# A two-layer encoder step on one core: down products added into DRAM by accumulating transfers, and stage ends by quarters of the tokens

## The chip, the cores and the metric

One core of a Trainium2 chip runs the whole program. The metric is the device time of one execution in microseconds, the median of several runs. TensorE (PE in the profile) multiplies, VectorE (DVE) and ScalarE (ACT) work elementwise and read the results from PSUM banks, GpSimd (POOL) does elementwise work and issues transfers, and SyncE (SP) issues transfers. Each engine executes its own instructions in order and waits on semaphores for the others.

## The reference

All data are fp32. There are 1024 new tokens of one stream and 32 of another, 1056 together, with a width of 1024.

```python
# layer 0
x = x + mixer(rmsnorm(x, a_norm))        # (gb * dwconv3(gc * u)) @ w_out
x = x + conv_ffn(rmsnorm(x, ffn_norm0))
# layer 1
k, v, logf = rmsnorm(x, kv_norm) @ w_kv   # shared keys, values, forget logits
x = x + fox_attention(rmsnorm(x, b_norm) @ w_q, k, v, logf) @ w_o
x = x + conv_ffn(rmsnorm(x, ffn_norm1))
y = rmsnorm(x, final_norm)

def conv_ffn(h):                          # d_ff = 2816
    g, v = split(dwconv3(h @ w_up), 2)    # causal depthwise convolution, width 3
    return (silu(g) * v) @ w_down
```

## The kernel before, in words

**Data.** The residual x is kept transposed, as eight tiles x[0..7] of 128 channels × 1056 tokens (`NK` = 8, `TT` = 1056). Tokens are cut in three ways: `CH`, three chunks of 352; `HALVES`, two of 528; `ENDS`, four quarters of 264. Each fp32 factor is split in a high part, rounded by ScalarE to the type that TensorE multiplies fast, and a low part, the difference, by VectorE. A product is three matmuls, high·high, high·low and low·high; `chain` (L167, matmuls L173 to L175) does them for a list of inner tiles. `bank` names PSUM: in the feed-forward stages two banks `d` of 512 and three banks `p` of 1024 columns. `keep`, `slot` and the pool for weights hand out SBUF; a tile is handed out again when its readers are done.

**Stages.** Mixer (`mixer`), feed-forward 0 (`ffn(0)`), attention (`attention`), feed-forward 1 (`ffn(1)`) run one behind the other. Norms are computed by `rstd` (L227): the sums of squares over channels by six small matmuls with a vector of ones (L238), a few operations on 88 × 3 numbers (L240 to L245), a diagonal `dg` (L247), a matmul that broadcasts it (L250) and a copy to `rstd` (L251). In the mixer and in attention the last down products call `summed`: for each tile of x and chunk the VectorE add (L321), the square (L224, ScalarE), its sum (L225, GpSimd, or VectorE for the last tile), and the spill of x to DRAM. The norm starts when the last tile is done.

**Feed-forward.** `begin` (L359) applies norm and gain to x by halves (L384), splits it (L374, L375), runs the first two tiles of the up product (L395), and forms the sums f1 to f4 of the quarters of x (L408 to L411) and their splits. From then on `pair` (L501) makes one gate tile and one value tile by seven products instead of eight (`product`, L498, 24 matmuls of 264 columns each, 168 in all); its operands are weights or sums of weights made by GpSimd (L523, L524, L532, L545) and split by `operand` (L487, L488). `act` turns a pair into an activation tile: halo copies by GpSimd (L287), a first convolution product by ScalarE (L296), two more by VectorE (L297, L298), silu (L567), product (L569) and split (L573, L574). There are 22 such tiles (`NF`).

**Down products.** x does not fit in SBUF during a feed-forward stage; it lies in DRAM as `xd`. After every two acts `stream` (L598) takes 24 steps, 8 tiles of x by 3 chunks. Each one loads a chunk of x (L607, on SP), does 6 matmuls, adds the result on VectorE (L610) and stores the chunk (L611, on SP). There are 5 slots `xs`. The steps of one group are set between the seven products of the next two `pair` calls, by a count of matmuls (L587); the last group is half left over when the last pair ends. Then x is loaded, and the last two acts are added by `down` (feed-forward 0) or `finish` (L257), which goes by quarters and writes the normed output. All transfers of weights, x and outputs stand in SP's one queue, in program order.

**Attention.** `weave` sets filler steps between the softmax work of each head; for the last head the fillers are 48 steps of the output product (`down_steps`) for the first six of eight head pairs, and the last two pairs follow.

## Time and profile before

| | us |
|---|---|
| median of 3 runs (lowest, highest) | 2775.31 (2773.56, 2778.65) |
| the profiled execution | 2773.91 |
| its span, first to last instruction | 2772.1 |
| TensorE busy | 2550.4 |
| VectorE busy | 1823.5 |
| ScalarE busy | 1057.2 |
| GpSimd busy | 473.7 |

The span is one execution as the profiler recorded it. "Busy" is the time in which an engine executed something; transfers that it issues and waits are not counted. PEclk is the clock that TensorE was granted, as a share of full speed. The page cuts the span in 40 equal slices and prints the busy share of each in tenths. A wait is named by the engine and line that waited, and by what released it.

### The profile page before, as it was taken

What the parts mean: (1) busy time and instruction counts of PE and PEld (TensorE: products, weight loads), DVE (VectorE), ACT (ScalarE), POOL (GpSimd) and SP (SyncE); (2) the same over time, 40 slices, a digit from 0 to 9 for tenths busy, and PEclk for the clock granted to TensorE, in tenths of its full rate; (3) what the DMA queues carried; (4) which work ended last, traced back from release to release, by engine and by line L of the source; (5) the groups of instructions that cost most, each with busy time, mean ns of one, the idle gap of its engine ahead of it and who ended that gap; (6) DMA issues with size and microseconds to landing.
All of it is one profiled execution on the core that took longest, in us unless ns stands there. A gap on an engine that the chain in (4) does not pass through costs nothing. (4 is left out here: it accounts for less than half of the span.)

```text
span 2772.1 us, 45529 instructions
## 1 busy us (share of the span) xinstructions
PE 2550.4 (92%) x17332; PEld 2471.8 (89%) x17332; DVE 1823.5 (66%) x3266; ACT 1057.2 (38%) x1850; POOL 473.7 (17%) x467
## 2 busy tenths in 40 slices
...
PEclk9999998999999999989999999999899999999997
...
GB/s 109 41 46 46 50 138 24 136 165 172 178 180 180 170 174 178 191 124 47 56 58 50 51 58 58 87 196 128 23 120 168 172 176 175 179 183 176 176 170 121
DMA packets 239786, 341.73 MB, mean 123 GB/s; under 512 B 31952, under 2 KB 195280, under 8 KB 239568
## 3 DMA queue, kind: packets, MB, share of 16 engines
...
## 5 line engine op out<-in xcount | busy, mean ns | idle before, releaser
L498 PE MATMUL pb_p<-b,wb 128*128 128x264 f32 x7056 | 951.1, 287 | 27.4 <-ACT u L530 14.8
L498 PEld LDWEIGHTS pb_p<-b,wb 128*128 128x128 f32 x7056 | 918.9, 190 | 31.8 <-ACT u L530 15.3
L610 DVE TENSOR_TENSOR xs<-xs,pb_d 128x352 f32<-128x352 f32 x480 | 246.9, 519 | 374.5 <-DMA xs<-xd 219.8
L173 PE MATMUL pb_d<-acth,wb 128*128 128x352 f32 (+1 forms) x992 | 331.6, 338 | 52.7 <-DVE xs L610 52.3
L175 PE MATMUL pb_d<-acth,wb 128*128 128x352 f32 (+1 forms) x992 | 326.3, 329 | 4.5 <-DVE wb L488 4.5
L174 PE MATMUL pb_d<-actl,wb 128*128 128x352 f32 (+1 forms) x992 | 324.9, 328 | 0.0
L173 PE MATMUL pb_d<-xh,wh 128*128 128x384 f32 (+2 forms) x864 | 287.4, 336 | 14.0 <-ACT xh L162 7.4
L174 PE MATMUL pb_d<-xl,wh 128*128 128x384 f32 (+2 forms) x864 | 285.6, 331 | 5.8 <-DVE xl L163 5.7
L175 PE MATMUL pb_d<-xh,wl 128*128 128x384 f32 (+2 forms) x864 | 284.8, 330 | 1.0 <-DVE wl L151 0.8
L487 ACT ACTIVATE wb<-wr 128x512 fp32r<-128x512 f32 x210 | 131.9, 628 | 359.5 <-PE pb_p L498 277.1
L173 PEld LDWEIGHTS pb_d<-acth,wb 128*128 128x128 f32 x992 | 190.4, 193 | 70.0 <-DVE xs L610 63.8
L487 ACT ACTIVATE wb<-ws 128x512 fp32r<-128x512 f32 x168 | 105.2, 627 | 295.4 <-PE pb_p L498 157.5
L523 POOL TENSOR_TENSOR ws<-wr 128x512 f32<-128x512 f32 x42 | 56.5, 1346 | 884.9 <-DMA wr<-in_w_up 438.0
L175 PEld LDWEIGHTS pb_d<-acth,wb 128*128 128x128 f32 x992 | 191.9, 193 | 6.2 <-DVE wb L488 6.2
L174 PEld LDWEIGHTS pb_d<-actl,wb 128*128 128x128 f32 x992 | 192.3, 194 | 0.2
L173 PEld LDWEIGHTS pb_d<-xh,wh 128*128 128x128 f32 x864 | 166.1, 193 | 20.0 <-ACT xh L162 7.9
L150 ACT ACTIVATE wh<-wraw 128x1024 fp32r<-128x1024 f32 (+1 forms) x71 | 74.3, 1046 | 275.8 <-PE pb_o L174 138.6
L174 PEld LDWEIGHTS pb_d<-xl,wh 128*128 128x128 f32 x864 | 166.7, 193 | 8.1 <-DVE xl L163 7.7
L175 PEld LDWEIGHTS pb_d<-xh,wl 128*128 128x128 f32 x864 | 166.3, 193 | 2.7 <-DVE wl L151 2.5
L488 DVE TENSOR_TENSOR wb<-wr,wb 128x512 fp32r<-128x512 f32 x210 | 161.8, 770 | 4.0 <-ACT wb L487 3.5
L296 ACT ACTIVATE y<-u,cv 128x1058 f32<-128x1058 f32 x96 | 108.5, 1175 | 80.8 <-POOL u L287 80.7
L859 DVE TENSOR_TENSOR pt<-pb_d,pt 128x512 fp32r<-128x512 f32 (+1 forms) x160 | 99.0, 632 | 60.4 <-ACT pt L858 59.3
(289 smaller groups left out, 4628.0 us busy)
## 6 DMA issues: line engine op xcount, KB each, us to landing
xs<-xd SPq DMA_DIRECT2D x480, 176.0 KB
xd<-xs SPq DMA_DIRECT2D x480, 176.0 KB
wr<-in_w_up SPq DMA_DIRECT2D x168, 256.0 KB
wr<-in_w_down SPq DMA_DIRECT2D x84, 256.0 KB
...
```

The lines of the kernel that those rows point to most:

```text
L150: nc.scalar.activation(h[:, i:j], raw[:, i:j], AF.Copy)
L173: nc.tensor.matmul(ps, wh, xh[:, c[0]:c[1]], start=(i == 0), stop=False)
L174: nc.tensor.matmul(ps, wh, xl[:, c[0]:c[1]], start=False, stop=False)
L175: nc.tensor.matmul(ps, wl, xh[:, c[0]:c[1]], start=False, stop=(i == n - 1))
L296: nc.scalar.activation(y, u[:, 0:TC], AF.Copy, scale=w[:, 0:1])
L487: nc.scalar.activation(t[:, 0], src, AF.Copy)
L488: nc.vector.tensor_sub(t[:, 1], src, t[:, 0].bitcast(F32))
L498: nc.tensor.matmul(ps[:, q, :QB], w[:, i, k], t[:, j, cs], start=(begin and k == 0 and n == 0), stop=(end and k == len(b) - 1 and n == 2), ...
L523: nc.gpsimd.tensor_add(s1, a21, a22)
L610: nc.vector.tensor_add(t, t, ps)
L859: nc.vector.tensor_sub(pt[:, 512:512 + n], ps[:, :n], pt[:, :n].bitcast(F32))
```

## The change

In the new code the parts are these.

- `xd` holds x by halves of 528 tokens, not by chunks of 352.
- `stream` no longer loads x. For each tile of x and each half it does two quarters: 6 matmuls of 264 columns into a bank, and a copy by ScalarE (L652) into a slot `xs`, of which there are now 3. After the second quarter GpSimd issues one transfer (L654) that adds the slot to the half of x in DRAM. A group has 32 steps; there are 9 groups in a layer.
- The last group of a layer has four acts. The pairs of tiles 20 and 21 have no filler steps between their products. `down` and `tokenwise` begin with products of the first three acts (`lag`) while the fourth is made.
- `tokenwise` replaces `summed` and `finish`: the last group of the mixer, of attention and of feed-forward 1 goes quarter by quarter through all tiles of x, with all its weights in SBUF (`resident`). The norm of a quarter is issued during the next one; that of the last quarter is kept (`self.rest`) and issued inside `begin`, at tile 5 of the first half. `normalise` applies norm and gain in place by quarters (L298).
- `begin` no longer applies the norm, and the sums of quarters of x are formed in the tiles of x (L436 to L438 on VectorE, L441 on GpSimd), all of one kind before the next.
- The last head of attention takes its blocks of queries in order, and has 24 filler steps, for the first four pairs; the last four pairs are added by `tokenwise`.

```diff
-        self.xd = [[self.dr.tile([128, c[1] - c[0]], F32, name=f"xd{m}{i}") for i, c in enumerate(CH)]
-                   for m in range(NK)]
+        self.xd = [[self.dr.tile([128, HB], F32, name=f"xd{m}{i}") for i in range(2)] for m in range(NK)]
...
     def spilled(self, m):
-        return zip(self.xd[m], (slice(*c) for c in CH))
+        return zip(self.xd[m], (slice(*c) for c in HALVES))
...
+    def tokenwise(self, weight, acts, x, after, hurry=False, lag=False):
+        g, banks = len(acts), self.singles()
         acc = self.keep("acc")
-        norm = self.rstd(acc, ENDS)
+        norm = self.rstd(acc, ENDS, True)
+        last = None
         for c in ENDS:
             cs, n = slice(*c), c[1] - c[0]
+            early = [next(banks)[:, :n] for _ in range(NK)] if lag and c is ENDS[0] else []
+            for m, ps in enumerate(early):
+                self.chain(ps, weight(m), acts, c, range(g - 1))
             for m in range(NK):
+                if m == NK - 2 and last:
+                    after(last, next(norm)[0])
+                ps = early[m] if early else next(banks)[:, :n]
+                self.chain(ps, weight(m), acts, c, range(g - 1, g) if early else None)
+                self.nc.vector.tensor_add(x[m][:, cs], x[m][:, cs], ps)
+                self.square_add(x[m][:, cs], acc[:, cs], m, hurry)
+                if not hurry:
+                    i = c[0] // HB
+                    self.nc.sync.dma_start(self.xd[m][i][:, c[0] - i * HB:c[1] - i * HB], x[m][:, cs])
+            last = c
+        if hurry:
+            after(last, next(norm)[0])
+        else:
+            self.rest = lambda: after(last, next(norm)[0])
+    def normalise(self, x, gain):
+        def f(c, r):
+            for m in range(NK):
+                xc = x[m][:, c[0]:c[1]]
+                self.nc.vector.scalar_tensor_tensor(xc, xc, self.gain[:, gain, m:m + 1], r, op0=OP.mult, op1=OP.mult)
+        return f
...
+    def resident(self, units):
+        ws = [self.weights(u, keep=i > 1) for i, u in enumerate(units)]
+        return lambda m: [tuple(t[:, m % 2 * 4 + k] for t in ws[m // 2]) for k in range(4)]
...
+    def down_steps(self, units, acts, x, done=None, lag=False):
+        nc, g = self.nc, len(acts)
+        tiles, early = {}, {}
+        banks = self.singles() if lag else iter(self.dbank, None)
...
+        def some(m, c, ks=None):
+            ps = early.setdefault((m, c), None)
+            if ps is None:
+                ps = early[m, c] = next(banks)[:, :c[1] - c[0]]
+            self.chain(ps, [wt(m * g + k) for k in range(g)], acts, c, ks)
+            return ps
+        for m in range(2 if lag else 0):
+            for c in CH:
+                some(m, c, range(g - 1))
         for m in range(NK):
-            w = [wt(m * g + k) for k in range(g)]
             for c in CH:
-                ps = self.dbank()
-                self.chain(ps[:, :c[1] - c[0]], w, acts, c)
-                nc.vector.tensor_add(x[m][:, c[0]:c[1]], x[m][:, c[0]:c[1]], ps[:, :c[1] - c[0]])
+                ps = some(m, c, range(g - 1, g) if (m, c) in early else None)
+                nc.vector.tensor_add(x[m][:, c[0]:c[1]], x[m][:, c[0]:c[1]], ps)
                 if done:
                     done(m, c)
                 yield
...
-    def summed(self, x):
...
-    def begin(self, x, acc, gain, units):
+    def begin(self, x, units):
...
         for i, c in enumerate(HALVES):
-            cs = slice(*c)
-            if i == 0:
-                next(norm), next(norm)
             ps = [self.bank("p").rearrange("p (q c) -> p q c", q=2) for _ in units]
             for m in range(NK):
-                nc.vector.scalar_tensor_tensor(x[m][:, cs], x[m][:, cs], self.gain[:, gain, m:m + 1], self.rs[:, cs],
-                                               op0=OP.mult, op1=OP.mult)
-                if i == 0 and m in (2, 4):
-                    next(norm)
+                if m == k2 + 1 and i == 0:
+                    self.rest()
                 n = "21"[m < k2] + "12"[i]
-                t = b[n][m % k2] = parts(x[m][:, cs], room(n != "12"))
+                t = b[n][m % k2] = parts(x[m][:, slice(*c)], room(n != "12"))
                 for p, (h, l) in zip(ps, ws):
                     w = (h[:, m], l[:, m])
                     for q in range(2):
...
+        one, two = (slice(*c) for c in HALVES)
         for k in range(k2):
-            b11, b12 = (x[k][:, slice(*c)] for c in HALVES)
-            b21, b22 = (x[k + k2][:, slice(*c)] for c in HALVES)
-            f = [self.slot("f", [128, 2, HB]) for _ in range(2)]
-            f1, f2, f3, f4 = f[0][:, 0], f[0][:, 1], f[1][:, 0], f[1][:, 1]
-            nc.vector.tensor_sub(f1, b12, b11)
-            nc.vector.tensor_sub(f2, b22, f1)
-            nc.gpsimd.tensor_sub(f4, f2, b21)
-            nc.vector.tensor_sub(f3, b22, b12)
-            for n, v in (("t2", f2), ("t3", f3), ("t1", f1), ("t4", f4)):
-                b[n][k] = parts(v, room(k == 0 or n in ("t1", "t2")))
+            p, q = x[k], x[k + k2]
+            nc.vector.tensor_sub(p[:, one], p[:, two], p[:, one])
+            nc.vector.tensor_sub(p[:, two], q[:, two], p[:, two])
+            nc.vector.tensor_sub(q[:, two], q[:, two], p[:, one])
+            b["t2"][k] = parts(q[:, two], room(False))
+        for k in range(k2):
+            nc.gpsimd.tensor_sub(x[k + k2][:, one], x[k + k2][:, two], x[k + k2][:, one])
+            b["t3"][k] = parts(x[k][:, two], room(k < 2))
+        for k in range(k2):
+            b["t1"][k] = parts(x[k][:, one], room())
+        for k in range(k2):
+            b["t4"][k] = parts(x[k + k2][:, one], room())
         return b, us
...
         acts = [act(0, *us)]
-        fill, n, at = iter(()), 0, 0
+        fill, n, at, many = iter(()), 0, 0, 4 * NK
         for t in range(1, NF):
-            if t % 2 == 0:
+            if t % 2 == 0 and t < NF - 2:
                 for _ in fill:
                     pass
-                fill, acts, n, at = self.stream(a["w_down"][l, t - 2:t], acts), [], 3 * NK, -2
+                fill, acts, n, at = self.stream(a["w_down"][l, t - 2:t], acts), [], many, -2
             us = []
             for _ in self.pair(a["w_up"][l, t], a["w_up"][l, NF + t], b, us):
                 at += 1
-                while n and (3 * NK - n) * (12 if t < NF - 2 else 24) < at * 3 * NK:
+                while n and (many - n) * 12 < at * many:
                     n -= 1
                     next(fill, None)
             acts.append(act(t, *us))
-        for _ in fill:
-            pass
         for m in range(NK):
             self.load(x, m)
-        (self.down if done else self.finish)(a["w_down"][l, NF - 2:], acts, x, *([done] if done else []))
+        units = a["w_down"][l, NF - 4:]
+        if done:
+            self.down(units, acts, x, done, True)
+        else:
+            ws = [self.operand(self.block(u, i), n % 2) for n, u in enumerate(units) for i in range(2)]
+            self.tokenwise(lambda m: [(ws[m][:, 0, k], ws[m][:, 1, k]) for k in range(4)], acts, x, self.result(x),
+                           True, True)
         nc.sync.dma_start(a["o_conv_f"][l], out)
...
     def stream(self, units, acts):
-        nc, g = self.nc, len(acts)
+        nc = self.nc
         for m in range(NK):
-            if m * g % 4 == 0:
-                w = self.operand(self.block(units[m * g // 8], m * g // 4 % 2))
-            i = m * g % 4
-            for c, d in zip(CH, self.xd[m]):
-                t = self.slot("xs", [128, c[1] - c[0]], F32, "xs", 5)
-                nc.sync.dma_start(t, d)
-                ps = self.bank("d")[:, :c[1] - c[0]]
-                self.chain(ps, [(w[:, 0, i + k], w[:, 1, i + k]) for k in range(g)], acts, c)
-                nc.vector.tensor_add(t, t, ps)
-                nc.sync.dma_start(d, t)
-                yield
+            if m % 2 == 0:
+                w = self.operand(self.block(units[m // 4], m // 2 % 2))
+            ws = [(w[:, 0, m % 2 * 2 + k], w[:, 1, m % 2 * 2 + k]) for k in range(2)]
+            for i, d in enumerate(self.xd[m]):
+                t = self.slot("xs", [128, HB], F32, "xs", 3)
+                for q in range(2):
+                    c = ENDS[2 * i + q]
+                    ps = self.bank("d")[:, :QB]
+                    self.chain(ps, ws, acts, c)
+                    nc.scalar.activation(t[:, q * QB:(q + 1) * QB], ps, AF.Copy)
+                    if q:
+                        nc.gpsimd.dma_start(d, t, accum_op=OP.add)
+                    yield
...
-        self.acts = [self.gather(NP - 2), self.gather(NP - 1, [b * 256 for b in ORDER[:2]])]
+        self.acts += [self.gather(NP - 2), self.gather(NP - 1, [b * 256 for b in self.order(HEADS - 1)[:2]])]
...
-        def outs(ps, first, done=None):
...
+        def outs():
+            with self.tc.issue_after(self.last[-3].ins):
+                acts = [self.gather(p) for p in range(4)]
+            for m in range(NK):
+                with self.tc.issue_after(self.last[-1].ins):
+                    self.load(x, m)
+            self.acts = [self.gather(p) for p in range(4, 6)]
+            yield from self.down_steps(a["w_o"][:4], acts, x)
...
         def fillers(h):
             if h == HEADS - 1:
-                def last():
-                    yield from outs(range(0, 4), 0)
-                    yield from outs(range(4, 6), 4)
-                return 6 * NK, last()
+                return 3 * NK, outs()
             p = h // 2 + 1
...
-        for _ in outs(range(6, 8), 6, done):
-            pass
+        self.tokenwise(self.resident(a["w_o"][4:]), self.acts, x, after)
...
-        "w_down": np.stack([down_units(w, (2,) * (NF // 2)) for w in i["w_ffn_down"]]),
+        "w_down": np.stack([down_units(w, (2,) * (NF // 2 - 2) + (4,)) for w in i["w_ffn_down"]]),
...
-        "w_o": down_units(i["w_o"][0], (4, 2, 2)),
+        "w_o": down_units(i["w_o"][0]),
```

Names and lines in what follows: of the program before, its own; of the changed program, its own.

**GpSimd in a steady part of feed-forward 0.** Before, one tile's work: weight sums into `ws` and halo copies `u<-cv`, `cv<-u`.

```order
L523 TENSOR_TENSOR ws<-wr 128x512
L524 TENSOR_TENSOR ws<-ws,wr 128x512
L291 COPY cv<-u 128x4
L532 TENSOR_TENSOR ws<-wr 128x512
L287 COPY u<-cv 128x2x2
L545 TENSOR_TENSOR ws<-wr,ws 128x512
L287 COPY u<-cv 128x2x2
```

Now, at the same place (`xd_77` and so on are halves of x in DRAM):

```order
L560 TENSOR_TENSOR ws<-wr 128x512
L561 TENSOR_TENSOR ws<-ws,wr 128x512
L330 COPY cv<-u 128x4
L654 DMA xd_77<-xs 128x528
L569 TENSOR_TENSOR ws<-wr 128x512
L654 DMA xd_78<-xs 128x528
L326 COPY u<-cv 128x2x2
L654 DMA xd_79<-xs 128x528
L326 COPY u<-cv 128x2x2
L330 COPY cv<-u 128x4
L582 TENSOR_TENSOR ws<-wr,ws 128x512
```

The issues of accumulating transfers, each of which waits for ScalarE's second copy into its slot, stand between the weight sums and the halo copies.

**ScalarE in the same part.** Before, from the first convolution products of an act to the high part of its result (`wb` are weight splits, `mid` a PSUM copy of `pair`):

```order
L296 ACTIVATE y<-u,cv 128x1058 x2
L487 ACTIVATE wb<-wr 128x512
L521 ACTIVATE mid<-pb_p 128x528
L487 ACTIVATE wb<-ws 128x512
L567 ACTIVATE y<-y 128x1058
L487 ACTIVATE wb<-ws 128x512
L487 ACTIVATE wb<-wr 128x512
L573 ACTIVATE acth<-y 128x1024
```

Now:

```order
L335 ACTIVATE y<-u,cv 128x1058 x2
L652 ACTIVATE xs<-pb_d 128x264 x2
L558 ACTIVATE mid<-pb_p 128x528
L524 ACTIVATE wb<-wr 128x512
L604 ACTIVATE y<-y 128x1058
L652 ACTIVATE xs<-pb_d 128x264 x2
L524 ACTIVATE wb<-ws 128x512
L610 ACTIVATE acth<-y 128x1024
```

The copies out of the down banks stand behind the convolution products and behind silu.

**VectorE at border 1, around the first half of `begin`.** Before, the last of the eight gains of the half (L384), a piece of the next norm (L241 to L243), and the splits (L375); `x_107` to `x_114` are the tiles of x:

```order
L384 SCALAR_TENSOR_TENSOR x_112<-x_112,gain,rstd 128x528
L384 SCALAR_TENSOR_TENSOR x_113<-x_113,gain,rstd 128x528
L384 SCALAR_TENSOR_TENSOR x_114<-x_114,gain,rstd 128x528
L241 TENSOR_SCALAR nw<-pb_d 88x3
L242 RECIPROCAL nr<-ne 88x3
L375 TENSOR_TENSOR b<-x_107,b 128x528
L375 TENSOR_TENSOR b<-x_108,b 128x528
L375 TENSOR_TENSOR b<-x_109,b 128x528
```

Now, where L283 is the add of a down product, L298 the gain of a quarter, L410 the split (`x_99` to `x_106` are the tiles of x):

```order
L283 TENSOR_TENSOR x_102<-x_102,pb_s 128x264
L410 TENSOR_TENSOR b<-x_99,b 128x528
L410 TENSOR_TENSOR b<-x_100,b 128x528
L283 TENSOR_TENSOR x_104<-x_104,pb_s 128x264
L410 TENSOR_TENSOR b<-x_101,b 128x528
L410 TENSOR_TENSOR b<-x_102,b 128x528
L410 TENSOR_TENSOR b<-x_103,b 128x528
L159 TENSOR_TENSOR wl<-wraw,wh 128x1024
L410 TENSOR_TENSOR b<-x_104,b 128x528
L410 TENSOR_TENSOR b<-x_105,b 128x528
L283 TENSOR_TENSOR x_103<-x_103,pb_s 128x264
```

The splits of the first half now stand among the last adds of the down products, and no gain of that half stands behind them.

102 lines of the change are left out of this document (42 added, 60 removed).

## Prediction

> **What bounds the kernel now.** I read the page's busy times first, then the windows that cover the stages, the table of waits, and last the groups inside single windows.
>
> ```profile
> span 2772.1 us, 45529 instructions
> PE 2550.4 (92%) x17332; PEld 2471.8 (89%) x17332; DVE 1823.5 (66%) x3266; ACT 1057.2 (38%) x1850; POOL 473.7 (17%) x467
> PEclk9999998999999999989999999999899999999997
> L610 DVE TENSOR_TENSOR xs<-xs,pb_d 128x352 f32<-128x352 f32 x480 | 246.9, 519 | 374.5 <-DMA xs<-xd 219.8
> ```
>
> TensorE is busy for 2550.4 of 2772.1 us, so at most 222 us can come back from its idle time, and some more from slices where the clock row is below 9. No other engine is near a bound of its own: the question is where TensorE stands still, and why.
>
> ```profile
> 395.00:500.00 105.00, 74.22 (x501) 70.82 (x500) 80.69 (x125) 44.85 (x78) 30.32 (x21) 0.84 0.17 55
> 500.00:1150.00 650.00, 630.86 (x4651) 624.42 (x4651) 442.50 (x716) 212.20 (x311) 133.42 (x154) 0.99 0.58 173
> 1150.00:1215.00 65.00, 49.00 (x233) 43.01 (x232) 42.10 (x58) 24.67 (x27) 21.10 (x12) 0.84 0.66 209
> 1895.00:2020.00 125.00, 89.38 (x569) 85.06 (x568) 92.27 (x146) 52.58 (x88) 43.05 (x24) 0.82 0.23 77
> 2050.00:2650.00 600.00, 579.68 (x4274) 572.10 (x4273) 404.90 (x657) 193.32 (x284) 121.76 (x142) 1.00 0.59 174
> 2680.00:2772.00 92.00, 54.76 (x287) 50.06 (x285) 50.68 (x112) 30.69 (x74) 21.57 (x26) 0.71 0.43 135
> 405.00:410.00 5.00, 2.10 (x9) 1.77 (x9) 2.78 (x9) 1.67 (x6) 0.00 (x0) 0.50 0.99 315
> 475.00:480.00 5.00, 0.00 (x0) 0.00 (x0) 5.00 (x5) 3.00 (x3) 3.20 (x2) 1.00 0.18 61
> 480.00:485.00 5.00, 2.61 (x12) 2.62 (x13) 3.33 (x7) 1.67 (x3) 1.94 (x2) 0.50 0.12 43
> ```
>
> A row is the window, its length, the busy us of TensorE, its weight loads, VectorE, ScalarE and GpSimd, TensorE's clock, the DMA share and GB/s. The six long windows are: border 1 (mixer to feed-forward 0), steady feed-forward 0, border 2 (to attention), border 3 (attention to feed-forward 1), steady feed-forward 1, and the finish. I count as lost the idle time plus busy time × (1 − clock), an upper bound for the clock's part. Border 1: 30.8 + 74.2 × 0.16 = 42.7. Border 2: 16.0 + 7.8 = 23.8. Border 3: 35.6 + 16.1 = 51.7. Finish: 37.2 + 15.9 = 53.1. Steady: 19.1 + 6.3 and 20.3 + 0, together 45.7. The three short windows show how an idle stretch costs twice: 405 to 410 and 480 to 485 run at 0.50, the latter right behind five us with no matmul.
>
> ```profile
> PE pb_d L173 <- DVE xs L610: 54.2, 58, 3.7
> DVE xs L610 <- DMA xs<-xd: 219.8, 126, 4.4
> SPq L607 <- DMA xd<-xs: 719.7, 367, 4.8
> ACT y L296 <- POOL u L287: 80.7, 48, 3.4
> ```
>
> In the steady parts TensorE waits 54.2 us for the adds L610 (both layers, partly outside my windows), the adds wait 219.8 us for loads of x, and SP's queue stands 719.7 us behind stores. So a round trip through DRAM in one in-order queue bounds those stretches, not arithmetic.
>
> **The stream, part by part.** A group is two tiles of up products and their down steps.
>
> ```profile
> 2451.80 0.32 PE L175 MATMUL pb_d<-acth,wb 128*128 128x352 f32 x1
> 2451.96 2.22 PE L498 MATMUL pb_p<-b,wb 128*128 128x264 f32 x17
> 2454.02 0.32 PE L173 MATMUL pb_d<-acth,wb 128*128 128x352 f32 x1
> L498 PE MATMUL pb_p<-b,wb 128*128 128x264 f32 x3290 | 442.4, 286 | 1.0 <-DVE wb L488 1.0
> wr<-in_w_up SPq DMA_DIRECT2D x168, 256.0 KB
> wr<-in_w_down SPq DMA_DIRECT2D x84, 256.0 KB
> ```
>
> A 352-wide matmul follows the last one after 2451.96 − 2451.80 = 0.16 us, a 264-wide after (2454.02 − 2451.96)/17 = 0.121. Three of the former cost 0.480, four of the latter 0.485: 0.005 × 48 per group × 18 groups = 4 us at most; I take +3. A group's matmuls are 2 × 168 × 0.121 + 192 × 0.121 = 64 us.
>
> *Removed:* 480 adds, loads and stores. *Added* per group: 32 copies on ScalarE and 16 accumulating transfers issued by GpSimd. The trace has the copy's shape in the norm:
>
> ```profile
> 2764.11 0.39 ACT L251 ACTIVATE rstd<-pb_d 128x264 f32<-128x264 f32 x1 [2.65 <-PE pb_d L250]
> L296 ACT ACTIVATE y<-u,cv 128x1058 f32<-128x1058 f32 x38 | 42.8, 1174 | 30.4 <-POOL u L287 30.4
> L523 POOL TENSOR_TENSOR ws<-wr 128x512 f32<-128x512 f32 x19 | 25.5, 1342 | 429.3 <-DMA wr<-in_w_up 233.0 <-DMA xd<-xs 173.5 <-DVE u L543 22.8
> L298 DVE SCALAR_TENSOR_TENSOR y<-u,cv,y 128x1058 f32<-128x1058 f32 x38 | 50.0, 1317 | 0.0
> ```
>
> 32 × 0.39 = 12.5 us per group. ScalarE is busy 212.2/650 = 33% of the steady window, 21 us of 64, and comes to 52%; VectorE falls from 68% (44 us) by 24 × 0.519 = 12.5 to 49%. Neither binds by its sum, but ScalarE works in order: the copies stand behind the two convolution products of an act (2 × 1.17 us), which wait for a GpSimd halo copy (80.7 us in 48 waits above, 3.4 at most), and that one now stands behind transfer issues. TensorE has two down banks, a step is due each 64/32 = 2.0 us, so about 4 us are covered. Mean block: 2.35 + 30.4/38 = 3.2, covered; worst: 2.35 + 3.4 = 5.75, a stall of 2 us. Over 36 acts that is 0 to 72 us; I take 0.7 each, 25, because the issues ahead of the halo push it toward the worse end. GpSimd also makes the weight sums (1.34 us each) between the same issues; a late sum holds TensorE in the up products, where only 1.0 us of idle time stood in the window. I give this 10 us (0 to 36, 1 us per act). What is late next, once loads of x are gone, is thus ScalarE's turn.
>
> *The accumulating transfer* is in no row, and no row has a transfer from GpSimd's queue. Bounds: the 405–410 row moved 315 GB/s at a share of 0.99, so 270 KB take 0.86 us of all 16 engines; it must read the destination as well, so at half that rate 1.7, at a quarter 3.4. Per group 12 weight blocks of 256 KB (252 over 42 tiles, 6 each) take 12 × 0.83 = 10 us, which leaves (64 − 10)/16 = 3.4 us for each. The second limit is the slot: three of them, a half each 4.0 us, so a slot must be back 12 us after its first copy, and the transfer may land up to 12 − 2.0 − 0.4 = 9.6 us after its issue.
>
> ```profile
> 2110.45 2.87 DMA xd<-xs
> 2132.61 3.45 DMA xd<-xs
> ```
>
> Such stores of 176 KB were 2.9 to 3.5 us on the chain; scaled by size 4.3 to 5.2, and doubled 8.6 to 10.4. So the nearest rows leave it hidden, with little to spare at the upper end. I take 0, and keep +230 us (below) as the far end. By the Trainium skill, "DMA: Bandwidth & Descriptors", "Anatomy of one DMA — SWDGE (gpsimd) path", a software-described transfer takes 2.0 us plus its bytes at 436 GB/s, here an estimated 2.6; by it the sum stays as it is. No run so far shows it. Stream: −45.7 + 3 + 25 + 10 = −8.
>
> **Border 1.** What moves: the norm of three of four quarters, square sums and stores of x run inside the last down products; x is stored by 32 quarter transfers in SP's queue in place of 24 thirds, and the first accumulation of the same address comes over 40 us later, so nothing waits there. What remains between the stages:
>
> ```profile
> L384 DVE SCALAR_TENSOR_TENSOR x<-x,gain,rstd 128x528 f32<-128x528 f32 x16 | 14.1, 955 | 5.5 <-ACT rstd L251 5.5
> L375 DVE TENSOR_TENSOR b<-f,b 128x528 fp32r<-128x528 f32 x16 | 14.1, 921 | 2.0 <-ACT b L374 1.9
> L375 DVE TENSOR_TENSOR b<-x,b 128x528 fp32r<-128x528 f32 x16 | 10.3, 701 | 0.0
> L408 DVE TENSOR_TENSOR f<-x 128x528 f32<-128x528 f32 x4 | 3.9, 973 | 0.0
> 2756.60 0.34 PE L175 MATMUL pb_d<-acth,wb 128*128 128x264 f32 x1
> 2760.13 1.04 PE L238 MATMUL pb_d<-ones,acc 128*88 128x1 f32 x6 [3.18 <-DVE acc L225]
> 2762.82 1.25 PE L250 MATMUL pb_d<-dg,ones 88*128 88x264 f32 x2 [1.66 <-DVE dg L247]
> 2764.53 3.48 DVE L278 SCALAR_TENSOR_TENSOR y<-x,gain,rstd 128x264 f32<-128x264 f32 x6 [1.76 <-ACT rstd L251]
> ```
>
> (a) Between the sum matmuls of a norm and its broadcast pass 2762.82 − 2760.13 = 2.7 us, in which TensorE finds little behind it in order: 3 us. (b) The last quarter's norm is deferred to the fifth tile of the first half, which leaves 3 tiles × 12 × 0.121 = 4.4 us of cover; from the broadcast on, 1.25 + 0.39, eight gains of 0.58 (3.48/6), two sums (0.97 each) and a split (some 0.6, by 0.39 for half its width, and 0.70) take 9.5: 5 us idle. (c) Over the second half (96 matmuls, 11.7 us) VectorE has 8 splits × 0.70, 12 sums × up to 0.97 and 8 splits of sums × 0.92 = 24.6 us ahead of or among the next weights' low parts, so up to 13 us of idle time if all stood ahead; about half do: 6. With 4 of clock, 18 remain of 42.7: −24. Were VectorE as full as now (80.7 of 105), only half of that.
>
> **Border 3** has the same steps, but the last four outputs of attention come late, and four weight units of 512 KB go through one raw buffer. 51.7 less 18 and 12 for that: −22. The last head gets 24 filler steps in place of 48:
>
> ```profile
> 1850.00:1895.00 45.00, 44.97 (x288) 43.95 (x289) 27.91 (x53) 10.59 (x20) 0.00 (x0) 1.00 0.23 61
> ```
>
> Now TensorE is full to the end of it, ScalarE nearly free: these last 45 us are steps left over behind the softmax, under which the outputs travel through DRAM. 24 steps of 6 × 0.16, 23 us, move behind it, and 22 of cover stay for the same journey. It should do; between 0 and 4.4, the longest wait for a load in the table of waits, I take +3.
>
> **Border 2.** The last group has four acts, and 6 chains of the first three run while act 21 is made: 6 × 9 × 0.16 = 8.6 us of cover. The act's own path has six VectorE operations of some 1.32 us (L298's row; four of the convolutions, a product, a low part) and two ScalarE products of 1.17, 10.3, and I estimate 2 us of hand-overs: 4 us idle, 2 of clock. Tiles 20 and 21 have no down steps between their products, so bank waits show; 3 us. Of 23.8 some 10 remain: −14.
>
> **Finish.** Now every quarter has 8 chains of 12 matmuls (11.6 us at full clock) in place of 6 (5.8), so VectorE's add and square sum (8 × (0.43 + 0.58) = 8.1) fit beneath them, which they don't now:
>
> ```profile
> L225 DVE TENSOR_TENSOR acc<-acc,sq 128x264 f32<-128x264 f32 x28 | 16.3, 583 | 2.7 <-ACT acc L221 1.0 <-ACT sq L224 0.5
> L269 DVE TENSOR_TENSOR x<-x,pb_d 128x264 f32<-128x264 f32 x16 | 6.8, 425 | 7.8 <-PE pb_d L175 7.7
> ```
>
> What stays is the end behind the last matmul, 2772.1 − 2756.9 = 15.2, of which the backlog of square sums gives 1; a gap of 5 before act 21; 3 in the norms, 3 in the unfilled tiles, 2 of clock. 28 of 53.1 remain, and since 53.1 is an upper bound I take −24 rather than −25.
>
> **Sum.** −8 − 24 − 22 + 3 − 14 − 24 = −89. The profiled execution took 2773.9 us, so 2685; the median of the runs shown is 1.4 above, hence 2686.
>
> **Rivals.** *The transfer gives its slot back too late* (slower). If it lands after 9.6 us, each half costs a third of the excess. At 12 us: 0.8 × 288 = +230, 2916. From 10.5 us (0.31 × 288 = 89) it eats the whole gain. For it: the destination is both read and written, the doubled store reaches 10.4, and GpSimd's queue has work in between. Against it: the DMA share in the steady window is 0.58 with 8.4 MB of x per group, and 4.3 MB stay.
>
> A rule weighs for this rival: the Trainium skill, "SBUF — State Buffer", in its box on the "DVE blocks DMA" trap, says that GpSimd cannot write a transfer's descriptors while VectorE runs certain operations (an fp32 copy is its example). The steady groups are two-input forms, not copies, and no run so far shows whether they count; if they did, two operations like L298 would add 2 × 1.32 us, to 6.9–7.8 for the scaled store and past 12 for the doubled one. By that rule alone the sum stays 2686 at the lower end and becomes this rival's at the upper.
>
> *VectorE still paces the borders* (faster, by half). It does the same gains, splits and sums, and is at 77% in the 395–500 window. Half of the 84 us of borders and finish are lost: 2686 + 42 = 2728.
>
> *The two queues stall in full*: 72 and 36 in place of 25 and 10, so 2686 + 73 = 2759. With the rival before it, 2801, slower. For it: one engine in order now carries the copies, the products and the weights' high parts. Against it: its mean wait for the halo is 0.8 us.
>
> *All goes well*: stalls at 0, three borders 3 us better each: 2686 − 35 − 9 = 2642.
>
> **How the numbers follow.** Forecast 0.52 (its own range 2655 to 2715, as the stream's stalls run from 0 to twice what I took). Half the borders 0.17, stalls in full 0.05, all well 0.06: faster 0.80. Slots late 0.12, both halves of the third rival 0.04: slower 0.16. No change 0.04, where gains and stalls meet; 0.2% (5.6 us) is about what a measurement of this kernel can tell from none. The range of 2640 to 2775 holds all but the slow cases and part of the best.
>
> **What would show it.** In the new profile: no load of x in the steady parts and SP idle there; TensorE at about 97% in a steady window, with its waits named by the copies; accumulating transfers below 9.6 us, the DMA share below 0.6. At border 1 idle pieces of 3, 5 and 6 us and none longer; at the finish 15 us behind the last matmul. Wrong would be: waits of the copies for their slots, a steady window below 94% busy, or GpSimd busy through the stream.

## The result, and the profile after

The changed kernel takes 2657.37 us, the median of 4 runs (2655.25 to 2663.52), against 2776.98 for the kernel before beside it. The ratio is 0.9572, with a 95% interval of 0.9551 to 0.9594: 120 us faster. I had forecast 2686 in a range of 2640 to 2775.

From the page of the changed kernel, the same rows as before, and the queue, the group, the landing and the waits of the new transfers:

```profile
span 2655.3 us, 46907 instructions
PE 2518.9 (95%) x18436; PEld 2463.4 (93%) x18436; DVE 1603.1 (60%) x2810; ACT 1259.8 (47%) x2468; POOL 731.2 (28%) x791
PEclk9999997999999999988999999999899999999998
q0 software_dynamic: 41472, 77.88, 22.2%
L654 POOL DMA_DIRECT2D xd<-xs x288 | 259.4, 901 | 502.3 <-ACT xs L652 494.1
xd<-xs POOLq DMA_DIRECT2D x288, 264.0 KB, 4.3
POOL xd L654 <- ACT xs L652: 494.1, 203, 3.9
ACT xs L652 <- PE pb_d L183: 307.0, 316, 2.9
```

The span is 116.8 us shorter. VectorE lost 220 us of work, ScalarE gained 203, and GpSimd 258, about the 259.4 us that its 288 issues take (0.90 us each; the page counts these as busy). A transfer lands 4.3 us after its issue, and the queue takes 22.2% of 16 engines' time. Nothing waits for a transfer for long: ScalarE's copies wait for TensorE, GpSimd for ScalarE.

Next, the steady parts. The bounds of these windows are the first matmuls of the products of tiles 2 and 20 in each layer, so both kernels do the same 18 tiles and 9 groups of down products between them. First the kernel before, then the changed one (columns as in the prediction):

```profile
490.30:1094.50 604.20, 585.06 (x4304) 578.89 (x4303) 410.24 (x661) 196.68 (x287) 125.62 (x144) 0.99 0.58 171
2019.20:2621.30 602.10, 582.71 (x4304) 575.78 (x4303) 408.04 (x660) 196.31 (x287) 123.73 (x144) 1.00 0.58 172
```

```profile
485.00:1061.30 576.30, 576.30 (x4731) 576.24 (x4730) 316.91 (x449) 294.79 (x571) 243.40 (x285) 1.00 0.67 116
1960.80:2537.30 576.50, 576.50 (x4730) 576.42 (x4729) 315.44 (x449) 294.42 (x571) 242.40 (x285) 1.00 0.67 116
```

604.2 and 602.1 us have become 576.3 and 576.5, and in the new rows TensorE is busy from end to end. Note the busy columns of the second rows, where the clock is 1.00 in both: 582.71 before and 576.50 now for the same matmul columns. So 6.2 us of the old loss stand inside that column. In the first rows the difference is 8.8 us, of which the old clock of 0.99 can account for up to 5.9.

Cut at such places in both traces (starts of first matmuls; the third cut is attention's first product of probabilities and values), the span divides so:

| stretch | before, us | after, us | difference | term of the prediction |
|---|---|---|---|---|
| start to tile 2 of feed-forward 0 (mixer, border 1) | 490.3 | 485.0 | −5.3 | −24 |
| tiles 2 to 20, both layers (the stream) | 1206.3 | 1152.8 | −53.5 | −8 |
| tile 20 to attention's first value product (border 2) | 186.9 | 167.0 | −19.9 | −14 |
| from there to tile 2 of feed-forward 1 (attention, border 3) | 737.8 | 732.4 | −5.4 | +3 − 22 |
| tile 20 of feed-forward 1 to the end (finish) | 150.8 | 118.0 | −32.8 | −24 |
| sum | 2772.1 | 2655.3 | −116.8 | −89 |

The sum is near, but two terms are far off, and in opposite directions: the stream gave 45 us more than I said, borders 1 and 3 some 32 less. The experiments ask why.

### The profile page after: what moved, and what is told of

It is laid out like the page before. It is cut to its first block, busy times and chain, and to the rows that moved or that the text cites. A ratio compares the mean times of both kernels' runs of the same rounds, so it can differ in the third digit from the quotient of the medians.

```text
span 2655.3 us, 46907 instructions
## 1 busy us (share of the span) xinstructions
PE 2518.9 (95%) x18436; PEld 2463.4 (93%) x18436; DVE 1603.1 (60%) x2810; ACT 1259.8 (47%) x2468; POOL 731.2 (28%) x791
## 3 DMA queue, kind: packets, MB, share of 16 engines
q0 software_dynamic: 41472, 77.88, 22.2%
q1 hardware_dynamic: 98736, 165.75, 20.7%
## 4 chain that ended last, share of the span: by engine, by line
PE 83%; DVE 8%; ACT 3%; issue 3%; DMA 2%; POOL 1%; SPq 0%; DVEq 0%; ACTq 0%; POOLq 0%
PE pb_p L535 31%; PE pb_d L181 12%; PE pb_d L182 12%; PE pb_d L183 12%; PE pb_o L888 2%; PE pb_s L181 2%; PE pb_s L183 2%; PE pb_s L182 2%; PE pb_d L899 1%; DVE pt L903 1%; PE pb_s L862 1%; PE pb_s L863 1%; PE pb_p L183 1%; PE pb_o L181 1%; PE pb_p L181 1%
## 5 line engine op out<-in xcount | busy, mean ns | idle before, releaser
L535 PE MATMUL pb_p<-b,wb 128*128 128x264 f32 x7056 | 948.3, 286 | 19.9 <-ACT mid L558 8.5
L535 PEld LDWEIGHTS pb_p<-b,wb 128*128 128x128 f32 x7056 | 900.6, 190 | 21.7 <-ACT mid L558 8.9
L654 POOL DMA_DIRECT2D xd<-xs x288 | 259.4, 901 | 502.3 <-ACT xs L652 494.1
L652 ACT ACTIVATE xs<-pb_d 128x264 f32<-128x264 f32 x576 | 218.7, 387 | 345.9 <-PE pb_d L183 307.0
L181 PE MATMUL pb_d<-acth,wb 128*128 128x264 f32 x1184 | 336.4, 285 | 0.0
L183 PE MATMUL pb_d<-acth,wb 128*128 128x264 f32 x1184 | 336.3, 284 | 0.0
L182 PE MATMUL pb_d<-actl,wb 128*128 128x264 f32 x1184 | 336.3, 284 | 0.0
L181 PEld LDWEIGHTS pb_d<-acth,wb 128*128 128x128 f32 x1184 | 222.8, 188 | 0.2
L182 PEld LDWEIGHTS pb_d<-actl,wb 128*128 128x128 f32 x1184 | 222.8, 188 | 0.1
L183 PEld LDWEIGHTS pb_d<-acth,wb 128*128 128x128 f32 x1184 | 222.8, 188 | 0.0
L181 PEld LDWEIGHTS pb_d<-xh,wh 128*128 128x128 f32 x864 | 167.1, 194 | 21.4 <-DVE pt L903 10.3
L525 DVE TENSOR_TENSOR wb<-ws,wb 128x512 fp32r<-128x512 f32 x168 | 127.5, 760 | 90.3 <-ACT wb L524 90.3
L336 DVE SCALAR_TENSOR_TENSOR y<-u,cv,y 128x1058 f32<-128x1058 f32 x96 | 123.4, 1321 | 75.0 <-ACT y L335 75.0
L233 POOL TENSOR_TENSOR acc<-acc,sq 128x264 f32<-128x264 f32 (+1 forms) x60 | 80.9, 1349 | 282.0 <-DMA xd<-x 131.7
```

The lines of the kernel that those rows point to most:

```text
L181: nc.tensor.matmul(ps, wh, xh[:, c[0]:c[1]], start=(i == 0), stop=False)
L182: nc.tensor.matmul(ps, wh, xl[:, c[0]:c[1]], start=False, stop=False)
L183: nc.tensor.matmul(ps, wl, xh[:, c[0]:c[1]], start=False, stop=(i == n - 1))
L233: (nc.vector if hurry or m == NK - 1 else nc.gpsimd).tensor_add(acc, acc, sq)
L336: nc.vector.scalar_tensor_tensor(y, u[:, 1:1 + TC], w[:, 1:2], y, op0=OP.mult, op1=OP.add)
L525: nc.vector.tensor_sub(t[:, 1], src, t[:, 0].bitcast(F32))
```

## The experiments

**Is the round trip what the stream gained?** In the changed kernel the stream gets its loads, adds and stores back, by halves, in SyncE's queue.

```diff
                 t = self.slot("xs", [128, HB], F32, "xs", 3)
+                nc.sync.dma_start(t, d)
...
-                    nc.scalar.activation(t[:, q * QB:(q + 1) * QB], ps, AF.Copy)
-                    if q:
-                        nc.gpsimd.dma_start(d, t, accum_op=OP.add)
+                    tq = t[:, q * QB:(q + 1) * QB]
+                    nc.vector.tensor_add(tq, tq, ps)
+                    if q:
+                        nc.sync.dma_start(d, t)
```

> The changed kernel with the old way back in its stream: each half of x is loaded by SyncE, two VectorE adds, stored by SyncE (3 slots), all else as changed. Theory A (the steady parts gained because x no longer makes a round trip through SyncE's queue; between the second and the twentieth tile the two layers gained 27.9 + 25.5 = 53 us): 2657 + 53 = 2710, between 2695 and 2730, with TensorE waiting again for VectorE's adds. Theory B (the round trip was hidden, and the steady parts gained because the last group of four acts took work out of them): 2657 to 2670.

The reverse: the kernel before with only the new stream.

> The kernel before with nothing but the new stream: x in DRAM by halves, ScalarE copies, accumulating transfers from GpSimd; borders, norms, last groups and attention as before. Theory A: 2777 - 53 = 2724, between 2712 and 2736. Theory B: 2765 to 2777.

Measured: 2669.82 us (ratio to before 0.9607, 0.9586 to 0.9627) for the round trip, and 2701.28 (0.9720, 0.9702 to 0.9737) for the stream alone. Their steady windows, the round trip's first:

```profile
484.70:1070.90 586.20, 580.10 (x4695) 575.10 (x4694) 411.05 (x724) 195.95 (x286) 116.42 (x143) 1.00 0.58 175
1966.60:2549.30 582.70, 577.11 (x4694) 573.28 (x4693) 410.47 (x724) 196.83 (x286) 116.15 (x143) 1.00 0.58 175
```

```profile
490.20:1066.80 576.60, 576.60 (x4730) 576.53 (x4729) 316.07 (x449) 294.77 (x571) 243.04 (x285) 1.00 0.66 116
1988.40:2564.80 576.40, 576.40 (x4729) 576.31 (x4729) 316.54 (x449) 294.79 (x571) 242.73 (x285) 1.00 0.66 116
```

With the stream alone both windows are as in the changed kernel, so theory B is out: the 53 us belong to the stream. In the rest it gave 13 us more at the finish, from tile 20 to the end (138.1 us against 150.8), and 6.7 at border 2 (180.2 against 186.9), because the last steps of the old stream lie behind the start of tile 20: from there to the end TensorE waited 13.1 us for the adds L610, and with the new stream 3.0 us for the copies. The whole is beyond theory A's range, on the better side. But the round trip costs only 9.9 + 6.2 = 16 us when it is put back, not 53. The accumulation is therefore not what most of the gain comes from, and theory A as I wrote it fell.

**What, then?** One thing that both of these kernels share is the halves: 16 transfers each way per group instead of 24. So: the kernel before, its round trip kept, by halves.

```diff
-        return zip(self.xd[m], (slice(*c) for c in CH))
+        return zip(self.xd[m], (slice(*c) for c in HALVES))
...
-            for c, d in zip(CH, self.xd[m]):
-                t = self.slot("xs", [128, c[1] - c[0]], F32, "xs", 5)
+            for i, d in enumerate(self.xd[m]):
+                t = self.slot("xs", [128, HB], F32, "xs", 3)
                 nc.sync.dma_start(t, d)
```

> The kernel before with its round trip kept (load and store by SyncE, VectorE adds, 3 slots), but by 16 halves of 264 KB in place of 24 thirds of 176 KB per group, and products of 264 columns; nothing accumulates. The round trip put back into the changed kernel cost its steady parts only 18.5 us of the 53 gained, so theory A does not carry the whole. Theory E (what cost was the number of round trips through one queue in order, 24 per group with each load behind an earlier store's landing): the other 34 us come back here without any accumulation, and the finish gains some of the 12.7 it gained with the new stream alone; span 2772 - 34 - 8 = 2730, between 2718 and 2742. Rival F (the round trip is cheap in the changed kernel because its other parts relieve SyncE's queue): no gain here, 2768 to 2780.

Measured: 2744.20 us, ratio 0.9896 (0.9867 to 0.9924). Its steady windows:

```profile
492.30:1075.10 582.80, 578.93 (x4695) 573.88 (x4693) 409.19 (x724) 197.05 (x286) 116.30 (x143) 1.00 0.58 176
2018.20:2604.50 586.30, 579.99 (x4695) 574.17 (x4694) 409.16 (x724) 196.88 (x286) 114.79 (x143) 1.00 0.57 174
```

They are 21.4 and 15.8 us shorter than before, 37 of the 53.5, near the 34 of theory E, with not one transfer accumulated and with 3 slots in place of 5. Accumulation then brings the other 16: this kernel's 1169.1 us fall to 1153.0 with the new stream, as the round trip's 1168.9 to 1152.8. Rival F is out. The whole is less good than theory E said: the profiled execution, the slowest of the four (2752.62 us), took 13.6 us more in attention from its first value product to its last (633.1 against 619.5), with no line of it edited; more on that at the end. The waits of SyncE's queue for the landing of stores did not shrink with the gain (875.8 us in 313 waits here, 719.7 in 367 before): they are longer and fewer. Nor did the adds' waits for loads:

```profile
DVE xs L612 <- DMA xs<-xd: 213.3, 123, 5.3
PE pb_d L172 <- DVE xs L612: 27.5, 34, 3.3
```

The adds stand nearly as long as before (219.8 us in 126 waits), and only what TensorE loses by it has halved (54.2 us before). So the gain came with the change to halves; whether it is the number of trips, or the products of 264 columns that came with them, was not parted.

**How near is the transfer to its limits?** Each accumulating transfer was issued a second time, to a spare place.

```diff
                         nc.gpsimd.dma_start(d, t, accum_op=OP.add)
+                        nc.gpsimd.dma_start(self.spare[m][i], t, accum_op=OP.add)
```

> The changed kernel with each accumulating transfer issued a second time, to a spare place in DRAM that nobody reads. The profile gives 22.2% of 16 engines' time for 288 transfers, 2.05 us of all engines each. Theory C (my bound of 3.4 us per half is real: the engines' busy time adds up): 16 x 4.1 + 10 = 76 us per group against 64, +12 x 18 = +210, 2867. Rival D (the packets' time is mostly waiting and overlaps, and a landing only has to beat 9.6 us): GpSimd's 16 further issues of 0.9 us are hidden, 2657 to 2680.

And the accumulation was left out: plain stores from the same queue.

```diff
-                        nc.gpsimd.dma_start(d, t, accum_op=OP.add)
+                        nc.gpsimd.dma_start(d, t)
```

> The changed kernel with plain stores in place of the accumulating transfers, same size, same queue (the addition to x is left out, so x in DRAM holds only the last group's share). Theory C/D agree that the transfer is hidden: 2657, within 5 us. If reading the destination is what costs, the queue's share of the engines falls from 22.2% to about 9% (0.86 us each, from the 315 GB/s row) and landing from 4.3 us to about 3; if the issue by software is what costs, both stay within a fifth of what they are.

Measured: 2685.69 us for twice (ratio 0.9662, 0.9637 to 0.9688), 2660.33 for plain stores (0.9571, 0.9546 to 0.9596). Rows of the page, for twice and with its windows, then for plain stores:

```profile
q0 software_dynamic: 82944, 155.75, 36.5%
xd<-xs POOLq DMA_DIRECT2D x288, 264.0 KB, 6.1
```

```profile
485.30:1072.90 587.60, 580.83 (x4731) 578.50 (x4729) 325.52 (x449) 290.96 (x571) 360.39 (x426) 1.00 0.97 178
1978.40:2566.00 587.60, 580.08 (x4713) 577.75 (x4711) 324.76 (x449) 289.85 (x567) 351.44 (x423) 0.99 0.96 175
```

```profile
q0 software_dynamic: 23040, 77.88, 7.5%
L654 POOL DMA_DIRECT2D xd<-xs x288 | 158.3, 550 | 558.3 <-ACT xs L652 548.7
xd<-xs POOLq DMA_DIRECT2D x288, 264.0 KB, 2.4
```

A plain store takes 0.075 × 2655.9 / 288 = 0.69 us of all engines, is issued in 0.55 us and lands after 2.4; with the addition 2.05, 0.90 and 4.3. So the price hangs on the addition and not on the issue by software, as the first of the two guesses had it. It triples the engines' time, more than the doubling that I took as the near bound and less than the quarter rate of the far one, and costs nothing as long as it is hidden. Twice fills the engines to a share of 0.97 and costs 11 us in each layer. Theory C said +210 and is wrong by its size, since the time per transfer isn't fixed: 0.365 × 2686.3 / 576 = 1.70 us under load, 3.40 per half, which is the very limit of 3.4. Rival D came nearer, 6 us above its range, but not by its reason: the engines are full. One accumulation is at 60% of the limit that I gave, and two are at it.

The size of the transfer, by quarters of 132 KB, and the number of slots:

```diff
-                    if q:
-                        nc.gpsimd.dma_start(d, t, accum_op=OP.add)
+                    nc.gpsimd.dma_start(d[:, q * QB:(q + 1) * QB], t[:, q * QB:(q + 1) * QB], accum_op=OP.add)
```

> The changed kernel with an accumulating transfer per quarter of 132 KB, 32 per group, in place of one per half. If the cost goes by bytes (2.05 us of all engines per half become 2 x 1.0, landing about 3): GpSimd issues 32 x 0.9 = 29 us per group instead of 14, its queue is 50 to 65% full, and the time is 2657 to 2675. If it goes by transfer (2.05 us and 4.3 us each whatever the size): 32 x 2.05 + 10 = 76 us per group, +12 x 18 = +210, 2867.

```diff
-                t = self.slot("xs", [128, HB], F32, "xs", 3)
+                t = self.slot("xs", [128, HB], F32, "xs", 2)
```

> The changed kernel with 2 slots xs in place of 3. A slot is held for the two quarters (2.0 us), the last copy (0.4), the issue (0.9) and the landing (4.3, median): 7.6 us, against 2 x 4.0 = 8.0. By my slot rule the steady parts then stand at their limit: 0 to +40 us, 2657 to 2697, as landings above the median no longer fit; if slots did not matter, 2657 within 5.

Measured: 2656.67 us for quarters (0.9561, 0.9532 to 0.9589) and 2670.04 for two slots (0.9609, 0.9581 to 0.9637). The page of the first, a window and a wait of the second:

```profile
q0 software_dynamic: 82944, 77.89, 25.8%
xd<-xs POOLq DMA_DIRECT2D x576, 132.0 KB, 3.8
```

```profile
484.50:1069.30 584.80, 579.87 (x4730) 577.04 (x4729) 314.67 (x449) 290.21 (x571) 237.73 (x285) 1.00 0.67 115
ACT xs L652 <- DMA xd<-xs: 202.0, 130, 4.3
```

The engines' time goes mostly by bytes: twice the transfers take 25.8% instead of 22.2%. The landing barely does, 3.8 us for half the size, and GpSimd's issue not at all (1.04 us for each). With two slots ScalarE waits 202 us for landings, and TensorE pays 8.5 and 6.4 us for it in the two layers. The slot rule of the prediction holds: 7.6 of 8.0 us is the edge.

**Why did the borders give so little?** The waits of TensorE in the changed kernel from 385 to 480 us, its longest rows on VectorE, and what stands at the third gap on GpSimd, ScalarE and TensorE:

```profile
PE pb_p L535 <- ACT mid L558: 4.1, 1, 4.1
PE pb_p L425 <- DVE b L410: 3.5, 1, 3.5
PE pb_s L181 <- DVE x L283: 2.9, 1, 2.9
PE pb_o L258 <- DVE dg L255: 2.6, 1, 2.6
```

```profile
396.80 4.49 DVE L298 SCALAR_TENSOR_TENSOR x<-x,gain,rstd 128x264 f32<-128x264 f32 x8
403.47 1.93 DVE L410 TENSOR_TENSOR b<-x,b 128x528 fp32r<-128x528 f32 x3
413.24 3.32 DVE L298 SCALAR_TENSOR_TENSOR x<-x,gain,rstd 128x264 f32<-128x264 f32 x8 [1.76 <-ACT rstd L259]
432.52 3.33 DVE L298 SCALAR_TENSOR_TENSOR x<-x,gain,rstd 128x264 f32<-128x264 f32 x8 [2.61 <-ACT rstd L259]
435.76 1.32 DVE L436 TENSOR_TENSOR x<-x 128x528 f32<-128x528 f32 x2
446.44 16.71 POOL L441 TENSOR_TENSOR x<-x 128x528 f32<-128x528 f32 x4 [17.39 <-DVE x L438]
446.44 12.80 POOL L441 TENSOR_TENSOR x<-x 128x528 f32<-128x528 f32 x1 [17.39 <-DVE x L438]
459.21 3.94 POOL L441 TENSOR_TENSOR x<-x 128x528 f32<-128x528 f32 x3
457.37 0.68 DVE L525 TENSOR_TENSOR wb<-ws,wb 128x512 fp32r<-128x512 f32 x1
463.31 1.18 ACT L335 ACTIVATE y<-u,cv 128x1058 f32<-128x1058 f32 x1 [7.65 <-POOL u L326]
467.17 11.63 PE L535 MATMUL pb_p<-b,wb 128*128 128x264 f32 x70 [4.12 <-ACT mid L558]
```

The gaps that I predicted are there, some 8, 5 and 7 us of idle time, and the first is longer than my 3: the splits of the first half (L410) and the gains of quarters (L298) stand on VectorE ahead of the last adds and of the third norm. At the second, eight gains and two sums (L436) run before the split that TensorE waits for. The third has a cause that I had not seen: GpSimd's four sums (L441) take 16.7 us where four took 9.5 before, the halo copy of the first act stands behind them, ScalarE behind the halo, and behind that the copy that TensorE waits for. Of the 16.7 us the first sum alone has 12.80; the other three take 1.3 each. The first begins while VectorE works without a pause on operations with two operands in SBUF, until 458.05, and ends 1.2 us behind them; the other three run beside an idle VectorE. So this gap too comes from VectorE's work.

All three look like an order that could be better. So I tried other orders. First, the sums and their splits behind the halo copies; then norm and gain of the second half tile by tile, each ahead of its split; then both, with the first half's splits behind the third norm. In the diffs `tailed` is the halo copy, `tile` the gain of one tile in both quarters of the half, `lows` the splits, `behind` the last split of the half, and `added` the diagonal of the third norm.

```diff
+        def fourth():
+            for k in range(k2):
+              with self.tc.issue_after(self.tailed.ins):
+                nc.gpsimd.tensor_sub(x[k + k2][:, one], x[k + k2][:, two], x[k + k2][:, one])
+            for k in range(k2):
+                b["t4"][k] = parts(x[k + k2][:, one], room())
...
         acts = [act(0, *us)]
+        fourth()
```

> The changed kernel with GpSimd's four sums (L441) and the splits made from them put behind the halo copies of the first act of each feed-forward stage. In the profile the sums take 16.7 us at border 1, ScalarE waits 7.65 us for the halo behind them, and TensorE 4.1 us for a copy behind that. Theory G (this order sets the third gap of the border): 4 to 6 us less at each of two borders, 2645 to 2650. Rival H (VectorE's sum of work paces the border): the gap is filled by the same work elsewhere, 2655 to 2660.

```diff
+                if i and m < 2:
+                    self.tile(m)
+                elif i:
+                    with self.tc.issue_after(lows[-2].ins):
+                        self.tile(m)
...
+            with self.tc.issue_after(behind):
                 nc.vector.tensor_sub(p[:, one], p[:, two], p[:, one])
```

> The changed kernel with norm and gain of the second half (quarters 2 and 3) applied tile by tile in one VectorE operation of 528 columns, each ahead of its own split, and the sums of quarters behind the last split. In the profile eight gains (3.3 us) and two sums (1.3) stand ahead of the first split of the second half, and TensorE idles 1.6 + 3.5 us there; eight other gains (3.3) stand ahead of the last add before begin. Theory G (order): 3 to 6 us less at each of two borders, 2645 to 2651. Rival H: 2655 to 2660, as the sums then come later and the third gap grows by what the second loses.

```diff
+                with self.tc.issue_after(self.added.ins):
                     t = b[n][m % k2] = parts(x[m][:, slice(*c)], room(n != "12"))
```

> The changed kernel with both of these, and with the splits of the first half put behind the third norm's diagonal on VectorE, so that the last adds of the down products and that norm are not behind them (TensorE waits 2.9 + 1.6 + 2.6 us there). Theory G: the three gaps shrink by 10 to 14 us at each of two borders, 2630 to 2640, and it beats both kernels. Rival H (VectorE is full from the last quarter to the second products, so order cannot win more than its idle time of about 10 us in that stretch): 2648 to 2657.

Measured: 2654.92, 2657.05 and 2654.01 us, with ratios of 0.9568 (0.9545 to 0.9591), 0.9582 (0.9559 to 0.9606) and 0.9567 (0.9544 to 0.9590): none can be told from the changed kernel. From the start to tile 2 they take 485.8, 489.3 and 486.4 us, where the changed kernel takes 485.0. Tile by tile shows best where the time went: its stretch from begin's first matmul to tile 1 fell from 35.4 to 30.6 us, and the next, to tile 2, rose from 32.6 to 42.0. The longest waits of the kernel with all of it, 385 to 485 us:

```profile
PE pb_p L553 <- ACT mid L576: 4.0, 1, 4.0
PE pb_p L553 <- DVE wb L543: 3.9, 2, 2.3
PE pb_p L553 <- ACT u L585: 3.1, 1, 3.1
```

The wait for VectorE's split (3.5 us) is gone, and waits in the products of tile 1 have taken its place. Theory G fell. Why the halo copies gained nothing by going ahead of the sums can be read on GpSimd, here in the kernel with the halo copies first and in the one with all of it:

```profile
452.63 5.17 POOL L326 COPY u<-cv 128x4 f32<-128x4 f32 x1 [23.98 <-ACT u L432]
445.19 10.90 POOL L330 COPY u<-cv 128x4 f32<-128x4 f32 x1 [19.77 <-ACT u L444]
```

A copy of four columns, 0.18 us for the next of its kind, took 5.17 and 10.90 us and ended within 0.1 us of the end of VectorE's unbroken run (457.76 and 456.04). The delay that the first sum had in the changed kernel fell on the halo copy. It is not so in every order: tile by tile the same sums took 1.7 to 1.8 us each beside VectorE, and VectorE's own among them took 1.8 in place of 0.7.

Then the work itself: the gains L298 were left out at both borders (the norm is still computed, but not applied).

> The changed kernel with the gains L298 left out (norm and gain are not applied to x at the two borders; the norm itself is still computed). Three orders of the same work left the borders where they were: from the start to the second tile 485.0, 485.8, 489.3 and 486.4 us. Theory H (VectorE's sum of work paces the border): 32 operations of 0.42 us less per border, 13.4 us, of which 8 to 13 come back at each of two borders: 2657 - 16 to 26 = 2631 to 2641, start to second tile 472 to 477. Rival I (the border is set by the clock's return to full speed and TensorE's own waits in order): under 3 us each, 2651 to 2660.

Measured: 2631.77 us, ratio 0.9476 (0.9453 to 0.9500). From the start to tile 2 it takes 477.6 us, 7.4 less than the changed kernel, and from attention's first value product to tile 2 of feed-forward 1 711.9, 20.5 less, of which 5.8 lie inside attention, where nothing was left out. So leaving out 13.4 us of VectorE's work per border brings back 7.4 and some 14.7. The total lies in theory H's range (2631 to 2641) and rival I is out, but the two borders lie on either side of its 8 to 13, and attention lent 5.8 us. The edit also takes out more than work: without the gains no split waits for a norm. At border 1 VectorE waited 2.61 us for `rstd` ahead of the last gains, and TensorE 3.5 us for the split behind them, which is 0.2 here; how much of the gain is the work and how much that wait was not parted. It is not right that VectorE is full at the border in the changed kernel: it is busy for 69.98 us of the window from 385 to 480.

```profile
385.00:480.00 95.00, 74.33 (x488) 71.03 (x487) 69.98 (x123) 42.14 (x81) 41.34 (x27) 0.82 0.19 58
```

Its work stands on the path in pieces, between waits for TensorE's sums and for ScalarE's copies, and what was put earlier in one piece was missing in the next, as the tile-by-tile order showed.

**Does running three acts ahead cover act 21?** Without it, at border 2 and at the finish:

```diff
-            self.down(units, acts, x, done, True)
+            self.down(units, acts, x, done, False)
...
-                           True, True)
+                           True, False)
```

> The changed kernel without lag: at border 2 and at the finish no chain of the first three acts is run ahead while act 21 is made. My prediction put 8.6 us of such chains beneath a path of some 12 us; by it both places lose their cover and some clock: +8 to +12 each, 2673 to 2681. Rival: the scheduler's order finds other work to put there, under +3 each, 2655 to 2663.

Measured: 2670.54 us, ratio 0.9610 (0.9589 to 0.9630). From tile 20 to attention's first value product it takes 176.7 us against 167.0, from tile 20 of the second layer to the end 120.7 against 118.0. One wait at border 2, without lag:

```profile
PE pb_d L181 <- ACT acth L610: 10.3, 1, 10.3
```

With lag, in the changed kernel:

```profile
PE pb_d L181 <- ACT acth L610: 0.9, 1, 0.9
```

So the early chains cover some 10 us at border 2, as I had it, and hardly anything at the finish, as the rival had it: there the wait for act 21 is 1.0 us even without them.

## Why the prediction was right or wrong

The forecast, faster to 2686 us, was right in sign and fell short by a quarter: −89 for −116.8. It came from terms whose errors partly cancel, and that the total is so near is in part luck.

*What bounds the kernel:* right in place. The steady parts lost what the round trip cost, and they lost more than I read from idle time and clock. In the two windows from tile 2 to 20 these show 25.0 + 19.4 = 44.4 us, and 53.5 were there to be had, since a part of the waits is inside the busy column.

*The stream, −8 against −53.5:* the largest miss, by mis-sized terms. I took 25 us for ScalarE's stalls and 10 for late weight sums; both are 0 in the new windows (576.30 busy of 576.30). I had put the mean block of 3.2 us beneath 4 us of cover, and then charged 0.7 us for each act in spite of it, on an argument (the issues push the halo toward the worse end) that no row carried. The +3 for narrower matmuls shows nowhere. I also laid the whole loss to the round trip as such, where halves without accumulation brought 37 of the 53. By the prediction's own windows, which reach past the start of tile 20, the miss is larger still: the stream alone also brought 6.7 us at border 2 and 12.7 at the finish, so −8 stands against some −73.

*The transfer:* right. The landing of 4.3 us is at the lower end of the scaled store's 4.3 to 5.2; the estimate of 2.6 us worked out from the Trainium skill, "DMA: Bandwidth & Descriptors", section "Anatomy of one DMA — SWDGE (gpsimd) path", is near the plain store's 2.4 and too low for an accumulating one. The limits of 3.4 us of engine time and of the slot were both met by a run that went up to them. The rival of late slots did not come; nor did the starved descriptors of the Trainium skill, "SBUF — State Buffer", box on the "DVE blocks DMA" trap: GpSimd's issue took 0.90 us and the landing 4.3, while VectorE ran mostly two-input forms for 316.91 of 576.3 us. For these forms the trace shows no such stall: 63 of the 288 issues lie wholly under VectorE operations on two SBUF operands, and took 0.86 to 0.90 us. One sign of the prediction failed: the DMA share of the steady windows is 0.67 and not below 0.6, since a transfer takes 2.05 us of the engines. In the rule that I weighed for the late slots, the doubled landing comes to 11.2 to 13.0 us and not past 12 throughout.

*Border 1, −24 against −5.3, and border 3:* wrong, and the rival named it. "VectorE still paces the borders" priced the loss at half; at border 1 it was four fifths. By the prediction's own measure 95 − 74.33 = 20.7 us of idle time and 74.33 × 0.18 = 13.4 for the clock remain in the window from 385 to 480, 34 where I said 18. The idle gaps are 8, 5 and 7 us and not 3, 5 and 6: the step that failed first is (a), whose wait I took for one norm alone, without VectorE's splits and gains ahead of it. The term most mis-sized is the clock, 4 us for 13: with three gaps in 80 us it is at 0.50 for 34 of the 95 us. And in (c) I did not see that VectorE's run would hold up GpSimd's first sum, and with it the halo copy, for 12.8 us.

For border 3 the figure of −5.4 has attention in it. From attention's last value product to tile 2 of feed-forward 1 the two kernels show, before first:

```profile
1900.93:2019.20 118.27, 83.81 (x528) 79.93 (x527) 87.94 (x139) 49.41 (x82) 43.05 (x24) 0.81 0.23 76
1831.83:1960.76 128.93, 103.33 (x745) 100.89 (x745) 86.58 (x164) 53.43 (x105) 48.07 (x42) 0.89 0.23 70
```

The new stretch has more products in it: 350 of 264 columns where 132 of 352 stood, 21 us more at 0.121 and 0.16 us each, because 24 filler steps moved behind the last head. For the same work it is thus some 11 us shorter, half of the −22, which is what the rival said. Idle time and clock by the prediction's measure fell from 50.4 to 37.0. The other part, between attention's first and last value products, is 16.0 us shorter with those 21 us gone from it, so it lost some 5 where I took 3; the drift told below is larger than either.

*Border 2, −14 against −19.9,* and *the finish, −24 against −32.8:* right in kind. The cover of 8.6 us was found to be some 10 at border 2 and hardly anything at the finish. Less what the stream alone had, 6.7 and 12.7 us, the new stage ends brought 13.2 and 20.1, near my 14 and 24. The end behind the last product did not stay at 15 us as I had it. The last product, the last norm's sums and broadcast, and the last gains of the changed kernel:

```profile
2636.50 0.28 PE L183 MATMUL pb_p<-acth,wk 128*128 128x264 f32 x1
2641.36 1.01 PE L246 MATMUL pb_d<-ones,acc 128*88 128x1 f32 x6 [0.80 <-DVE acc L233]
2645.79 1.22 PE L258 MATMUL pb_d<-dg,ones 88*128 88x264 f32 x2 [3.42 <-DVE dg L255]
2647.53 3.51 DVE L311 SCALAR_TENSOR_TENSOR y<-x,gain,rstd 128x264 f32<-128x264 f32 x6 [1.89 <-ACT rstd L259]
```

From the end of that matmul, 2636.8, to the end of the span pass 18.5 us: the third quarter's norm is still under way there, and only 4.6 us later does the last one's begin.
